# Column-tiled adaLN units placed behind the reads of the sample states

## The chip, the core and the metric

One NeuronCore of a Trainium2 chip runs the whole program. The metric is the device time of one execution in microseconds (us). TensorE is called PE, VectorE DVE, ScalarE ACT, GpSimd POOL; SP is the engine whose queue issues nearly all DMAs, in program order.

## The reference, cut to what matters

One decoder layer for 256 prompt tokens and 8 sample sequences of 8 tokens, all in float32:

```
mod = silu(c) @ w_ada + b_ada                        # adaLN: 9 rows of c, 6 x 2048 columns
h   = rmsnorm(x) * (1 + scale1) + shift1
proj = h @ w_in                                      # feeds both branches
GLA: S_t = diag(a_t) S_{t-1} + k_t^T v_t,  o_t = q_t S_t        # 4 heads, states 256 x 512
SSD: h_t = exp(dt_t A) h_{t-1} + dt_t x_t B_t^T,  y_t = h_t C_t # 8 groups, states 128 x 512
x = x + gate1 * ((sigmoid(gA) * yA + sigmoid(gB) * yB) @ w_mix_out)
x = x + gate2 * SwiGLU(rmsnorm(x) * (1 + scale2) + shift2)
```

The samples start from given states, so each of the 8 sequences has its own state per head or group, which is read (q S, or C h), updated and written back.

## The kernel before, in words

**Weights.** Every large product runs as "quads": a tile of 512 x 512 weights is loaded in two halves (`raw`, 512 KB each, `load_raw` line 162), split into a rounded part `whi` (ACT) and the rest `wlo` (DVE, `split_w` line 172), and multiplied in 48 matmuls of 320 columns: for each 128 x 128 block `whi` by the high and by the low part of the activations, then `wlo` by the high part (`quad_mm`, line 327). `raw` has 4 buffers, `whi` and `wlo` 3 each. `Stream.ahead` splits two halves ahead of the one in use.

**The order of the work.** PE's order is the order in which the program is written. Small work runs from generators: `Background.tick` (line 144) is called 8 times per quad, once after every 6 matmuls, and `yield n` lets n ticks pass before the next step. The order of the other engines and of SP is made by the compiler's scheduler, which also hands out the buffers as they come free. `bg.drain()` (line 894 for GLA, 1119 for SSD) runs what is left of a generator at once.

**adaLN units.** `mod` is made in units (class `Ada`, line 248). A unit loads 1 MB of `w_ada` into two of the four `raw` buffers (`load`) and multiplies it with `c` as the stationary operand, 32 columns wide, so that four matmuls of 512 columns run side by side in four column groups of the array (`mm`, line 274; tile `ad`). After four units ACT copies the sums to `adap`, and `flush` (line 294) transposes them with PE (tile `p`) and adds them up on DVE into `mod`. 36 units run at the start, 60 between quads from line 912 on: `ada_every[0] = 2` lets every second quad load one unit at its start and run it at its end. The last four run before the feed-forward part.

**Sample states.** Class `States` (line 599) has 10 buffers `st` of 256 KB. `read` multiplies four states with four stationary operands of 32 columns, in the same four column groups (tile `inter`); `update` runs one matmul (tile `upd`), adds it to the state on DVE and stores the state. `gla_work` (line 626) does four reads per head, each followed by four updates, a step every second tick; `ssd_work` (line 956) does two reads per group in the same way. The GLA part has 4 heads and runs beside the products of lines 882 to 908; the SSD part has 8 groups, whose work starts beside the z product of its group.

The profile shows one float32 matmul as two instructions, so that a read or a unit of four matmuls is "x8" there and "x4" in the program's order.

Of the kernel before, what the change touches and what calls it, by code (L numbers as in the profile page):

```python
# [60 lines left out]
def hybrid_kernel(tc, ctx, a, o):  # L61
# [14 lines left out]
    def stile(shape, dt=F32, name="s"):  # L76
        t = pool.tile(shape, dt, tag="s", bufs=N_S, name=name)
        return t
# [26 lines left out]
    def tt(eng, out, in0, in1, op):  # L105
        return eng.tensor_tensor(out=out, in0=in0, in1=in1, op=op)  # L106
# [141 lines left out]
    class Ada:  # L248
# [12 lines left out]
        def load(self, small=False, spare=False):  # L261
            if self.units:
# [8 lines left out]
                    raws = [load_raw(src[:, h * 1024:(h + 1) * 1024], spare or c < 8) for h in range(2)]  # L271
                self.loaded.append((c, b0, nb, q, raws))

        def mm(self):
            self.flush()
            if not self.loaded:
                return
            c, b0, nb, q, raws = self.loaded.pop(0)
            if q == 0:
                t = psum.tile([128, 512], F32, tag="ad", bufs=1, name="ad")  # L280
                self.ps = t
            w = 128 * nb
            m = 2048 // w
            n = m // len(raws)
            for j in range(m):
                T.matmul(self.ps[32 * (j % 4):32 * (j % 4) + 32, :w], c_s[:, m * q + j, :],
                         raws[j // n][:, (j % n) * w:(j % n) * w + w], start=q == 0 and j < 4,
                         stop=q == nb - 1 and j >= m - 4, tile_position=(0, 32 * (j % 4)))
            if q == nb - 1:
                part = stile([128, 512], name="adap")  # L290
                S.copy(part[:, :w], self.ps[:, :w])
                self.parts.append((c, b0, nb, part))
# [26 lines left out]
    ada = Ada()  # L319
# [29 lines left out]
    quad_no = [0]  # L349
    ada_every = [0]  # L350

    def gemm(names, quads, evac, apart=False):
        pss = [mm_ps() for _ in range(4)]
        n = len(names)
        for q in range(n):
            quad_no[0] += 1
            xq = quads(q) if callable(quads) else quads[q]
            quad_mm(pss, names[q], xq, q == 0, q == n - 1, evac,
                    1 if ada_every[0] and len(ada.units) > 4 and quad_no[0] % ada_every[0] == 0 else 0, apart,
                    (lambda: quads(q + 1)) if callable(quads) and q + 1 < n else None)  # L360


# [141 lines left out]
    def stack_k(ps, hf, n):  # L504

        R = pool.tile([96, n, 128], F32R, tag="k", bufs=3, name="R")
        src = ps[quarter(hf), 0:128 * n].rearrange("p (a b) -> p a b", a=n)
        S.copy(R[quarter(0)], src)
        S.copy(R[quarter(1)], src)
        tt(V, R[quarter(2)], src, R[quarter(hf)].bitcast(F32), ALU.subtract)  # L510
        return [stack_stationary(R[:, i]) for i in range(n)]
# [114 lines left out]
    def gla_work(H):  # L626
        hd, vT, KK, qe, kx = H.hd, H.vT, H.KK, H.qe, H.kx
        order = [(4 * hf + j, kb) for hf in range(2) for kb in range(2) for j in range(4)]
        states = States([a["S_gla"][hd, b, kb] for b, kb in order], [o["gla_s"][hd, b, kb] for b, kb in order])
        yield 6 if hd else 12  # L630
        states.load(4)
        yield 4

# [6 lines left out]
            T.transpose(ps[0:64, 128 * mb:128 * mb + 128], vT[:, mb, NP:], ident)  # L640
        S.copy(xs_tok[0:64], ps[0:64])
        hst = [stack_k(psK, hf, 2) for hf in range(2)]
        yield 4

        psA = ax_ps("inter")
        for n in range(4):
            hf, kb = divmod(n, 2)
            if kb == 0:
                mv = stack_v(xs_tok, hf)
            states.read(psA, [H.qpad[:, kb, 4 * hf + j] for j in range(4)], n, n == 0, n == 3)  # L650
            yield 1
            for j in range(4):
                tok = NP + 8 * (4 * hf + j) + 7

                def decay(st, ps, kb=kb, tok=tok):
                    V.scalar_tensor_tensor(out=st, in0=st, scalar=H.eb[:, kb, tok:tok + 1], in1=ps,
                                           op0=ALU.mult, op1=ALU.add)

                states.update(n, j, hst[hf][kb][:, j], mv, decay)
                yield 1  # L660
        inter = stile([128, 512], name="inter")
        S.copy(inter, psA)
        vt = []
# [245 lines left out]
    prev = heads[3]  # L909


    ada_every[0] = 2

    def conv_evac(ck, dst, cvs, cvo):
        def f(mb, pss):
# [31 lines left out]
    def bc8(x):  # L947
        return x.unsqueeze(2).to_broadcast([x.shape[0], 8, 64])

    def v8(x):  # L950
        return x.rearrange("p (h d) -> p h d", d=64)
# [4 lines left out]
    def ssd_work(W):  # L956
# [29 lines left out]
        xl = stile([64, 512], name="xl")  # L986
        tt(V, v8(xl), v8(ps[0:64]), bc8(dtL_tok[:, hsl]), ALU.mult)
        tt(V, v8(xs_tok[0:64]), v8(ps[0:64]), bc8(dt_tok[0:64, 2, hsl]), ALU.mult)
        yield 4

        psA = ax_ps("inter")
        for hf in range(2):
            mv = stack_v(xl, hf)
            states.read(psA, [cpad[:, 4 * hf + j] for j in range(4)], hf, hf == 0, hf == 1)
            for j in range(4):
                st = states.tiles[4 * hf + j]
                tt(G, v8(st), v8(st), bc8(ecs[:, :, 4 * hf + j]), ALU.mult)
            yield 1
            for j in range(4):
                states.update(hf, j, hst[hf][:, j], mv, lambda st, ps: tt(V, st, st, ps, ALU.add))  # L1000
                yield 1
        inter = stile([128, 512], name="inter")
        tt(V, v8(inter), v8(psA), bc8(ecs_r[:, hsl]), ALU.mult)

# [415 lines left out]
```

## Time and profile before

| | |
|---|---|
| median of 3 runs | 2940.89 us (2935.99 to 2942.86) |
| the profiled execution | 2946.89 us, its span 2945.1 us |
| PE busy | 2881.8 us, 98% of the span |
| PE weight loads busy | 2690.5 us |
| DVE, ACT, POOL busy | 1581.7, 1266.9, 360.3 us |
| mean granted TensorE clock | 0.994 |
| moved by DMA | 575.55 MB, mean 195 GB/s |

A matmul's record is longer than the step from one to the next, since matmuls overlap: a product of 320 columns is shown with 0.31 us and starts every 0.147 us. Costs on PE are therefore read as differences of start times. "Idle before" in a row begins only when the matmul before it has ended by its record.

### The profile page before, as it was taken

The numbers are of one execution on the slowest core, as the hardware profiler recorded it, in microseconds if no ns is written. First come the engines' busy times: TensorE is split into PE (matmuls) and PEld (weight loads), VectorE is DVE, ScalarE is ACT, GpSimd is POOL, SyncE is SP. The second block draws the span as 40 slices with busy tenths as digits, with TensorE's granted clock in tenths as the row PEclk, the third lists the DMA queues.
The fourth block names the chain that finished last, engine by engine and source line by source line (L and its number), as shares of the span: only waits on it lengthen the run. The fifth ranks groups of instructions, "written<-read, shape, count | busy, mean of one in ns | idle before, by whom it ended". The sixth has DMA issues, their size and how long they took to land.

```text
span 2945.1 us, 48524 instructions
## 1 busy us (share of the span) xinstructions
PE 2881.8 (98%) x19594; PEld 2690.5 (91%) x19594; DVE 1581.7 (54%) x2302; ACT 1266.9 (43%) x1991; POOL 360.3 (12%) x516
## 2 busy tenths in 40 slices
PE   7999999999999999999999999999999999999998
PEld 5898888998888889888888999999999999999998
DVE  5565565656656666666566544446344443444445
ACT  4344544345554554545455333435333233323333
POOL 0002111212322232322223000000000000000000
PEclk9999999999999999999999999999999999999999
DMA  9846636747667575775756644464444444444443
GB/s 386 323 137 236 203 134 209 233 161 275 239 213 241 202 252 192 240 238 201 243 195 238 210 167 161 168 217 138 150 151 150 149 149 150 149 150 150 151 150 115
DMA packets 181113, 575.55 MB, mean 195 GB/s; under 512 B 23252, under 2 KB 24600, under 8 KB 180888
## 3 DMA queue, kind: packets, MB, share of 16 engines
q1 hardware_dynamic: 180888, 572.45, 56.9%
q8 instruction: 154, 2.52, 0.3%
q14 instruction: 71, 0.58, 0.1%
HBM read 528.63 MB, written 43.74 MB: 194 GB/s over the span
## 4 chain that ended last, share of the span: by engine, by line
PE 86%; DMA 5%; DVE 5%; ACT 2%; issue 1%; SPq 0%; POOL 0%; ACTq 0%; DVEq 0%; POOLq 0%
PE mm L115 77%; DMA raw<-w_in 3%; PE ad L115 3%; DVE wlo L106 2%; ACT whi L132 1%; PE y L115 1%; PE fin L115 1%; PE upd L115 1%; DMA raw<-w_sp 1%; PE inter L115 1%; PE o L115 1%; DVE cacc L931 1%; DMA csb<-cs_d 1%; PE sum L115 0%; PE att L115 0%
## 5 line engine op out<-in xcount | busy, mean ns | idle before, releaser
L106 DVE TENSOR_TENSOR wlo<-raw,whi 128x1024 fp32r<-128x1024 f32 x712 | 883.1, 1242 | 949.6 <-ACT whi L132 934.6
L132 ACT CAST whi<-raw 128x1024 fp32r<-128x1024 f32 x712 | 746.0, 1048 | 1336.9 <-PE mm L115 1006.3
L115 PE MATMUL mm<-hh,whi 128*128 128x320 f32 x2560 | 812.4, 317 | 7.3 <-ACT whi L132 4.6
L115 PE MATMUL mm<-hh,wlo 128*128 128x320 f32 x2560 | 793.8, 310 | 9.3 <-DVE wlo L106 9.1
L115 PE MATMUL mm<-hl,whi 128*128 128x320 f32 x2560 | 791.8, 309 | 1.3 <-DVE hl L106 1.3
L115 PEld LDWEIGHTS mm<-hh,whi 128*128 128x128 f32 x2560 | 481.9, 188 | 86.1 <-issue 50.7
L115 PEld LDWEIGHTS mm<-hh,wlo 128*128 128x128 f32 x2560 | 481.9, 188 | 12.4 <-DVE wlo L106 12.1
L115 PEld LDWEIGHTS mm<-hl,whi 128*128 128x128 f32 x2560 | 482.5, 188 | 9.6 <-issue 2.9
L115 PE MATMUL mm<-gh,whi 128*128 128x320 f32 x1408 | 435.4, 309 | 0.8 <-ACT gh L1242 0.8
L115 PE MATMUL mm<-gl,whi 128*128 128x320 f32 x1408 | 435.6, 309 | 0.0
L115 PE MATMUL mm<-gh,wlo 128*128 128x320 f32 x1408 | 435.3, 309 | 0.0
L115 PEld LDWEIGHTS mm<-gh,whi 128*128 128x128 f32 x1408 | 264.3, 188 | 1.8 <-ACT gh L1242 1.8
L115 PEld LDWEIGHTS mm<-gl,whi 128*128 128x128 f32 x1408 | 264.3, 188 | 0.5 <-DVE gl L106 0.3
L115 PEld LDWEIGHTS mm<-gh,wlo 128*128 128x128 f32 x1408 | 264.3, 188 | 0.0
L115 PE MATMUL mm<-alo,whi 128*128 128x320 f32 x704 | 217.6, 309 | 0.0
L115 PE MATMUL mm<-ahi,whi 128*128 128x320 f32 x704 | 217.6, 309 | 0.0
L115 PE MATMUL mm<-ahi,wlo 128*128 128x320 f32 x704 | 217.6, 309 | 0.0
L106 POOL TENSOR_TENSOR ss<-ss,sq 128x320 f32<-128x320 f32 x14 | 12.1, 867 | 1410.6 <-ACT sq L109 1410.6
L115 PE MATMUL mm<-yhi,whi 128*128 128x320 f32 x512 | 171.6, 335 | 5.2 <-DVE yb L106 4.7
L115 PE MATMUL mm<-yhi,wlo 128*128 128x320 f32 x512 | 158.2, 309 | 0.0
L115 PE MATMUL mm<-ylo,whi 128*128 128x320 f32 x512 | 158.1, 309 | 0.0
L115 PEld LDWEIGHTS mm<-ahi,whi 128*128 128x128 f32 x704 | 132.2, 188 | 0.0
(279 smaller groups left out, 3635.1 us busy)
## 6 DMA issues: line engine op xcount, KB each, us to landing
raw<-w_in SPq DMA_DIRECT2D x320, 512.0 KB, 4.1
raw<-w_fi SPq DMA_DIRECT2D x176, 512.0 KB, 3.6
raw<-w_ada SPq DMA_DIRECT2D x120, 512.0 KB, 5.5
raw<-w_fo SPq DMA_DIRECT2D x88, 512.0 KB, 3.5
raw<-w_sp SPq DMA_DIRECT2D x64, 512.0 KB, 4.6
araw<-w_ada SPq DMA_DIRECT2D x52, 512.0 KB, 8.6
st<-S_gla SPq DMA_DIRECT2D x64, 256.0 KB, 5.0
gla_s<-st SPq DMA_DIRECT2D x64, 256.0 KB, 3.5
```

Source lines behind the costliest of these rows:

```text
L106: return eng.tensor_tensor(out=out, in0=in0, in1=in1, op=op)
L115: Tensor.last = nc.tensor.matmul(*args, **kw)
L132: first = S.copy(hi, src)
L931: V.scalar_tensor_tensor(out=av[:, 0:344], in0=u[:, k:k + 344], scalar=vec[:, cw + k:cw + k + 1], in1=av[:, 0:344], op0=ALU.mult, op1=ALU.add)
```

## The change

After each read of sample states one adaLN unit runs at once, in the GLA part too, where no unit ran before: 4 in each of the 4 heads and 2 in each of the 8 SSD groups, 32 in all. A new method `preload` loads a unit a few ticks ahead of the first read of a head or group, and the next unit directly behind the unit just run. `unit` is `mm` without the flush in front; the flush comes behind the first update that follows. The remaining 28 units run after every fourth quad in place of every second, and only when no preloaded unit waits. The updates of GLA take one tick more per read, those of SSD three ticks each in place of two; the GLA work of heads 1 to 3 begins four ticks earlier.

```diff
--- before.py
+++ after.py
@@ -271,8 +271,15 ...
                     raws = [load_raw(src[:, h * 1024:(h + 1) * 1024], spare or c < 8) for h in range(2)]
                 self.loaded.append((c, b0, nb, q, raws))
 
+        def preload(self):
+            if len(self.units) > 4 and not self.loaded:
+                self.load()
+
         def mm(self):
             self.flush()
+            self.unit()
+
+        def unit(self):
             if not self.loaded:
                 return
             c, b0, nb, q, raws = self.loaded.pop(0)
@@ -356,7 +363,7 ...
             quad_no[0] += 1
             xq = quads(q) if callable(quads) else quads[q]
             quad_mm(pss, names[q], xq, q == 0, q == n - 1, evac,
-                    1 if ada_every[0] and len(ada.units) > 4 and quad_no[0] % ada_every[0] == 0 else 0, apart,
+                    1 if ada_every[0] and len(ada.units) > 4 and quad_no[0] % ada_every[0] == 0 and not ada.loaded else 0, apart,
                     (lambda: quads(q + 1)) if callable(quads) and q + 1 < n else None)
 
 
@@ -627,7 +634,7 ...
         hd, vT, KK, qe, kx = H.hd, H.vT, H.KK, H.qe, H.kx
         order = [(4 * hf + j, kb) for hf in range(2) for kb in range(2) for j in range(4)]
         states = States([a["S_gla"][hd, b, kb] for b, kb in order], [o["gla_s"][hd, b, kb] for b, kb in order])
-        yield 6 if hd else 12
+        yield 2 if hd else 12
         states.load(4)
         yield 4
 
@@ -640,6 +647,7 ...
             T.transpose(ps[0:64, 128 * mb:128 * mb + 128], vT[:, mb, NP:], ident)
         S.copy(xs_tok[0:64], ps[0:64])
         hst = [stack_k(psK, hf, 2) for hf in range(2)]
+        ada.preload()
         yield 4
 
         psA = ax_ps("inter")
@@ -648,6 +656,9 ...
             if kb == 0:
                 mv = stack_v(xs_tok, hf)
             states.read(psA, [H.qpad[:, kb, 4 * hf + j] for j in range(4)], n, n == 0, n == 3)
+            ada.unit()
+            if n < 3:
+                ada.preload()
             yield 1
             for j in range(4):
                 tok = NP + 8 * (4 * hf + j) + 7
@@ -657,7 +668,9 ...
                                            op0=ALU.mult, op1=ALU.add)
 
                 states.update(n, j, hst[hf][kb][:, j], mv, decay)
-                yield 1
+                if j == 0:
+                    ada.flush()
+                yield 2 if j == 0 else 1
         inter = stile([128, 512], name="inter")
         S.copy(inter, psA)
         vt = []
@@ -909,7 +922,7 ...
     prev = heads[3]
 
 
-    ada_every[0] = 2
+    ada_every[0] = 4
 
     def conv_evac(ck, dst, cvs, cvo):
         def f(mb, pss):
@@ -986,19 +999,25 ...
         xl = stile([64, 512], name="xl")
         tt(V, v8(xl), v8(ps[0:64]), bc8(dtL_tok[:, hsl]), ALU.mult)
         tt(V, v8(xs_tok[0:64]), v8(ps[0:64]), bc8(dt_tok[0:64, 2, hsl]), ALU.mult)
+        ada.preload()
         yield 4
 
         psA = ax_ps("inter")
         for hf in range(2):
             mv = stack_v(xl, hf)
             states.read(psA, [cpad[:, 4 * hf + j] for j in range(4)], hf, hf == 0, hf == 1)
+            ada.unit()
+            if hf == 0:
+                ada.preload()
             for j in range(4):
                 st = states.tiles[4 * hf + j]
                 tt(G, v8(st), v8(st), bc8(ecs[:, :, 4 * hf + j]), ALU.mult)
             yield 1
             for j in range(4):
                 states.update(hf, j, hst[hf][:, j], mv, lambda st, ps: tt(V, st, st, ps, ALU.add))
-                yield 1
+                if j == 0:
+                    ada.flush()
+                yield 2
         inter = stile([128, 512], name="inter")
         tt(V, v8(inter), v8(psA), bc8(ecs_r[:, hsl]), ALU.mult)
 
```

**PE, at the first read of the GLA part** (`inter` is a read, `mm` the weight matmuls, `ad` the unit). One piece of the difference:

```order
 L115 MATMUL mm<-hh,wlo 128x320
 L115 MATMUL inter<-st,qpad 32x512 x4
+L115 MATMUL ad<-raw,c_s 32x512 x4
 L115 MATMUL mm<-hh,whi 128x320
 L115 MATMUL mm<-hl,whi 128x320
```

The unit now stands directly behind the read. Counted over the whole order, column-tiled stretches that other matmuls enclose (reads, units, or both joined) go from 121 to 93; four of the joined ones were there before.

**SP, around the first read of SSD group 1** (`raw<-w_ada` is half a unit, `raw<-w_in` half a weight tile, `st` the states, `csb` a table of 640 KB that this group needs). Before:

```order
L167 DMA raw<-w_ada 128x1024
L936 DMA conv_o<-cvo 128x108
L610 DMA st<-S_ssm 128x512 x4
L967 DMA csb<-cs_d 128x1280 x2
L167 DMA raw<-w_ada 128x1024
L167 DMA raw<-w_in 128x1024 x2
L610 DMA st<-S_ssm 128x512 x4
L167 DMA raw<-w_in 128x1024 x2
```

And now:

```order
L949 DMA conv_o<-cvo 128x108
L617 DMA st<-S_ssm 128x512 x4
L980 DMA csb<-cs_d 128x1280 x2
L167 DMA raw<-w_in 128x1024
L167 DMA raw<-w_ada 128x1024 x2
L167 DMA raw<-w_in 128x1024
L167 DMA raw<-w_ada 128x1024
L617 DMA st<-S_ssm 128x512 x4
L167 DMA raw<-w_ada 128x1024
L167 DMA raw<-w_in 128x1024
```

Both halves of the unit now stand behind the tables and behind one weight half; the next unit and four states stand ahead of a later weight half. In the even groups the weight half that here stands right behind `csb` stands ahead of the states, where half a unit stood before.

**SP, between the second and the third read of GLA head 1** (`gla_s` are stores of states). Before:

```order
L624 DMA gla_s<-st 128x512
L610 DMA st<-S_gla 128x512 x4
L624 DMA gla_s<-st 128x512
L526 DMA d_3383<-d 128x320
L167 DMA raw<-w_in 128x1024
L624 DMA gla_s<-st 128x512
```

And now:

```order
L631 DMA gla_s<-st 128x512
L617 DMA st<-S_gla 128x512 x4
L167 DMA raw<-w_ada 128x1024 x2
L631 DMA gla_s<-st 128x512
L167 DMA raw<-w_in 128x1024
L631 DMA gla_s<-st 128x512 x2
```

A unit's 1 MB now stands between the states and the next weight half.

## Rows read from the trace of the kernel before

**Rows 1.** The page: span, and busy time of each engine (share of the span, instructions).

```profile
span 2945.1 us, 48524 instructions
...
PE 2881.8 (98%) x19594; PEld 2690.5 (91%) x19594; DVE 1581.7 (54%) x2302; ACT 1266.9 (43%) x1991; POOL 360.3 (12%) x516
```

**Rows 2.** Who waited for whom, PE, from 680 to 1600 us (the SSD part): total us, times, longest.

```profile
PE mm L115 <- DVE wlo L106: 9.1, 10, 1.5
...
PE mm L115 <- ACT whi L132: 4.6, 6, 1.4
```

**Rows 3.** The same, from 200 to 680 us (the GLA part): the longest of all, and the longest of a weight product.

```profile
PE sum L115 <- POOL ss L106: 2.0, 1, 2.0
...
PE mm L115 <- ACT ohi L132: 1.1, 1, 1.1
```

**Rows 4.** PE in order of time, at the first GLA read: start us, us, instruction.

```profile
239.59 0.31 PE L115 MATMUL mm<-hh,wlo 128*128 128x320 f32 x1
239.83 1.06 PE L115 MATMUL inter<-st,qpad 128*32 128x512 f32 x8
240.82 0.41 PE L115 MATMUL mm<-hh,whi 128*128 128x320 f32 x1
241.07 0.30 PE L115 MATMUL mm<-hl,whi 128*128 128x320 f32 x1
```

**Rows 5.** The same, at the first unit behind a quad.

```profile
630.40 0.31 PE L115 MATMUL mm<-hh,wlo 128*128 128x320 f32 x1
630.64 1.07 PE L115 MATMUL ad<-raw,c_s 128*32 128x512 f32 x8
631.63 0.41 PE L115 MATMUL mm<-hh,whi 128*128 128x320 f32 x1
631.88 0.30 PE L115 MATMUL mm<-hl,whi 128*128 128x320 f32 x1
```

**Rows 6.** The same, at the first read of SSD group 1, which a unit followed directly (in brackets: idle before, and what ended it).

```profile
801.59 0.31 PE L115 MATMUL mm<-hh,wlo 128*128 128x320 f32 x1
801.83 1.06 PE L115 MATMUL inter<-st,cpad 128*32 128x512 f32 x8
802.71 1.04 PE L115 MATMUL ad<-raw,c_s 128*32 128x512 f32 x8
804.85 0.41 PE L115 MATMUL mm<-hh,whi 128*128 128x320 f32 x1 [1.10 <-ACT whi L132]
...
806.22 0.42 PE L115 MATMUL mm<-hh,wlo 128*128 128x320 f32 x1 [0.81 <-DVE wlo L106]
```

**Rows 7.** The loads of the stationary operand of units: ns min/median/max, first and last start us, forms.

```profile
L115 PEld LDWEIGHTS ad<-raw,c_s x480: 106/109/111, 630.6 to 1678.6; 128*32 128x32 f32 x160
```

**Rows 8.** ACT in order of time, at the same read of SSD group 1.

```profile
803.75 1.04 ACT L132 CAST whi<-raw 128x1024 fp32r<-128x1024 f32 x1 [0.69 <-PE ad L115]
805.06 1.04 ACT L132 CAST whi<-raw 128x1024 fp32r<-128x1024 f32 x1 [0.27 <-DMA raw<-w_in]
```

**Rows 9.** SP in order of time, ahead of it (the time is that of the issue alone).

```profile
792.69 0.90 SPq L967 DMA_DIRECT2D csb<-cs_d  x2
793.69 0.38 SPq L167 DMA_DIRECT2D raw<-w_ada  x1
794.46 1.43 SPq L167 DMA_DIRECT2D raw<-w_in  x2
795.94 3.00 SPq L610 DMA_DIRECT2D st<-S_ssm  x4
```

**Rows 10.** DMA issues from 794.4 to 795.7 us: KB each, median us from issue to landing.

```profile
raw<-w_in SPq DMA_DIRECT2D x2, 512.0 KB, 9.3
```

**Rows 11.** The page: the two instructions that split a weight half (busy us, mean ns of one, idle before).

```profile
L106 DVE TENSOR_TENSOR wlo<-raw,whi 128x1024 fp32r<-128x1024 f32 x712 | 883.1, 1242 | 949.6 <-ACT whi L132 934.6
L132 ACT CAST whi<-raw 128x1024 fp32r<-128x1024 f32 x712 | 746.0, 1048 | 1336.9 <-PE mm L115 1006.3
```

**Rows 12.** DMA issues from 228 to 284 us (the reads of GLA head 0): KB each, median us to landing.

```profile
raw<-w_in SPq DMA_DIRECT2D x9, 512.0 KB, 6.3
```

**Rows 13.** The same from 430 to 490 us (head 2).

```profile
raw<-w_in SPq DMA_DIRECT2D x13, 512.0 KB, 4.7
```

**Rows 14.** Busy time by stretch: the stretch, its us, busy us of PE, its weight loads, DVE, ACT, POOL, granted clock, share of the DMA engines' time, GB/s. The first is between two reads of head 0, the second between two of head 1, the last two are other stretches of heavy loading.

```profile
250.77:261.72 10.95, 10.95 (x73) 9.71 (x73) 5.61 (x7) 2.14 (x3) 0.00 (x0) 1.00 0.93 322
...
348.70:359.70 11.00, 11.00 (x74) 9.72 (x74) 8.64 (x12) 4.38 (x9) 0.00 (x0) 1.00 0.80 263
...
20.00:60.00 40.00, 36.68 (x295) 28.26 (x288) 20.15 (x39) 21.22 (x41) 0.52 (x1) 0.96 1.02 400
...
803.70:806.30 2.60, 0.69 (x7) 0.38 (x3) 1.47 (x2) 2.09 (x2) 2.60 (x3) 1.00 1.07 406
```

**Rows 15.** PE in order of time, an update and the weight matmul behind it.

```profile
242.68 0.40 PE L115 MATMUL upd<-mv,hs 96*128 96x512 f32 x1
242.92 0.31 PE L115 MATMUL mm<-hh,whi 128*128 128x320 f32 x1
```

**Rows 16.** The updates of the GLA states on DVE: ns min/median/max, first and last start us.

```profile
L656 DVE SCALAR_TENSOR_TENSOR st<-st,ge,upd x64: 740/747/749, 243.7 to 595.5; 128x512 f32<-128x512 f32 x64
```

## What the change should do, written before it ran

> **What bounds the kernel now.** Read first the page: PE is busy for 98% of the span, DVE for 54% [rows 1]. Only what PE does, or waits for, can move the time. Second, read who waited for whom. In the SSD part PE waits for split weights, 9.1 us for `wlo` and 4.6 us for `whi` in 16 waits, none over 1.5 us [rows 2]; in the GLA part no weight product waits for more than 1.1 us [rows 3]. Third, read PE in order of time where it leaves the weight matmuls. A lone read costs more than its own work: the last weight matmul ahead of it starts at 239.59, the second behind it at 241.07, which is 1.48 us for two ordinary steps of 0.147 and the read, so 1.19 us [rows 4]. A lone unit costs the same, 630.40 to 631.88 [rows 5]. Where a unit follows a read directly, it starts 0.88 us after the read [rows 6], and not after the 0.99 us plus a slow step that weight matmuls need. The change in and out of the column-tiled form is paid once for both.
>
> **The profiled execution.** It took 2946.9 us, 6.0 above the median of 2940.9. Terms are summed against the former; the forecast is the median plus the sum.
>
> **Term 1, joining: -8.7 us.** Joined, read and unit take 0.24 (into the read) + 0.88 + 0.99 (unit to the next weight matmul) + 0.25 (to the second), less two steps of 0.147: 2.07 us [rows 4 to 6]. Apart they take 2 x 1.19 = 2.38. One join saves 0.31 us. The order holds 32 joined pairs; 4 stood there before, and in 4 more only a flush lay between, so column-tiled stretches go from 121 to 93. 28 x 0.31 = 8.7 us, all on PE, which nothing covers. The number of units, and with it what they load, stays.
>
> The four column groups share their rows, and a load of a unit's stationary operand takes 109 ns [rows 7]; the unit at 802.71 began 0.88 us after its read, as two passes of the read take, so its first four loads ran beside the read [rows 6]. The Trainium skill, "TensorE: Matmul & The Clock Gate", Part 3, The mechanism, says against this that weight loads run beside matmuls in flight only where their row groups differ. The trace does not bear that out here; what it would cost is rival (d).
>
> **Term 2, units in the GLA part: +3 us.** Sixteen units come to where none ran. Their PE time only moves here from later. What is new is that from the first preload of a head to its last unit, some 45 us, two of the four `raw` buffers belong to units, and weight halves go through the other two. In the order a weight half that takes a buffer which a unit gives back is used 48 to 60 matmuls and three updates later: 48 x 0.147 + 3 x 0.24 = 7.8 us at least [rows 15]. It needs a landing, 4.7 us by the median in head 2 and 6.3 in head 0 [rows 12, 13], a `whi` of 1.05 and a `wlo` of 1.24 [rows 11]: 7.0 to 8.6 us. The spare time is -0.8 to +0.8 us, where the kernel before had four buffers and no such wait [rows 3]. One half per head is worse placed: its load stands behind the store of a state, which waits for an update's 0.75 us on DVE [rows 16], and 7.0 us are left. I take one late half of 0.75 us per head, 3 us. The ends are 0 (all land as in head 2) and 16 x 0.8 = 13 us (all as in head 0).
>
> The DMA engines are what sets those landings. Between two reads of head 0 they are 93% busy, so 10.2 of 10.95 us, in head 1 80% [rows 14]. A unit adds 1 MB, 2.6 us at the 400 GB/s of heavy loading [rows 14]. The interval grows by the unit's 0.88 us on PE and one tick, 6 x 0.147 = 0.88, to 12.7; that tick uses a quarter of a weight half, 0.3 us more of loading. So the engines are needed for 13.1 of 12.7 us at the fullest, and for 8.8 + 2.9 = 11.7 at a common interval: at the bound in the one, a microsecond short of it in the other. Neighbours share a queue, so I add nothing for it here; it is rival (b).
>
> **Term 3, the first read of an SSD group: +3.8 us.** Before, in group 1, the weight matmul behind read and unit starts at 804.85 where 802.71 + 0.99 = 803.70 was possible, and the third of them at 806.22, another 1.07 late [rows 6]. Together 2.2 us, where the rows show 1.10 + 0.81 idle. The reason is the queue: unit half, two weight halves and four states are issued behind two `csb` tables [rows 9], the two weight halves land 9.3 us after their issue [rows 10], and their splits start as they land, at 803.75 and 805.06, one landing every 1.31 us [rows 8]. Scaled by 2.2 / 1.9, the 13.7 us of rows 2 are some 15.8 us on PE.
>
> Now one weight half stands first behind `csb` and lands at about 802.4, the two unit halves at 803.7 and 805.0. Weights are no longer late, but the unit is: it could start at 802.71, its second half must wait until 805.0, so it is 2.3 us late. The next unit and four states then stand ahead of a later weight half: 805.0 + 1.3 (a weight half) + 1.3 (half a unit) + 2.6 (states) + 1.3 (the other half) + 1.3 = 812.8; split by 812.8 + 1.05 + 1.24 = 815.1. It is wanted 9.8 us after the read plus the 2.3, at 813.9, and its `wlo` 0.3 later: 0.9 us late. In even groups the first weight half stands ahead of the states, so each unit half lands a step sooner: 1.25 us late, then some 0.4. After: 4 x 3.2 + 4 x 1.65 = 19.4 us, against 15.8: +3.6, and 0.2 for flushes that now come closer behind their unit. The ends: if every landing comes a step of 1.3 us sooner, only the odd groups' units are late, 4 x 1.0, which is -11.8; a step later in every group is 8 x 1.3 more, +14.
>
> **Term 4, the rest: +0.4 us.** The loop of head 0 is four ticks longer without an earlier start, so its last update falls into the drained stretch behind it. It moves 0.24 us of PE and 0.75 of DVE there [rows 15, 16]; 0 to 0.75. The wider updates cost PE nothing: each is the same matmul, and DVE has room. The SSD work ends a quad later, still ahead of its drain. Fewer units beside the other quads save nothing, since nothing waited there.
>
> **Sum.** -8.7 + 3 + 3.8 + 0.4 = -1.5 us: 2939.4. About 0.2% (5.9 us) is what a measurement of this kernel tells from no change.
>
> **Rivals.** (a) *The weights keep up.* Landings stay near 4.7 us in GLA and the SSD queue costs what it cost before. Then only terms 1 and 4 count, -8.3: 2932.6; with part of the SSD waits gone, 2930. For it: DVE has room, and beside the units of ordinary SSD quads two free buffers were enough, since rows 2 show only 16 waits in 920 us. Against it: the 9.3 us landings [rows 10]. Chance 0.33. (b) *The transfers bound the GLA reads* (the side of slower). Where the DMA engines need longer for an interval than PE, every weight half comes later by the excess. It decides where they move this mixture at the rate of the fullest interval, 322 / 0.93 = 346 GB/s, and not at 400: 1.18 MB then cost 3.4 us, the interval 13.6, 0.9 more than PE needs, and landings go to those of head 0 or beyond. Term 2 is then its end of 13, term 3 stays: +8.5, 2949.4. For it: 93% busy already [rows 14]. Against it: heads 1 to 3 have more room, and less than half of the intervals are that full. Chance 0.18. (c) *What I forecast*, the joins paid back by late units and late weights: 0.47. (d) *A unit's loads wait for the read.* Then a join exposes 4 x 0.109 = 0.44 us and saves 0.31, so term 1 is 28 x 0.13 = +3.6, the sum +10.8, 2951.7. Only rows 6 speak on it, and against it: 0.02.
>
> That the joins do not happen is no rival: the order shows them.
>
> **How the numbers follow.** The likeliest is (c), 2939.4, by its own terms 2934 to 2946. The range takes in (a) to 2930 and most of (b): 2930 to 2950. Faster by over 0.2% is (a), 0.33; within 0.2%, (c), 0.47; slower, (b) and (d), 0.20. All terms at their lower or all at their upper ends together I leave out.
>
> **What would show it.** Right: a unit starting 0.4 us or more after its place behind an SSD read while its `raw` lands; no more lone reads; first weight matmuls behind SSD reads that don't wait; some waits for `whi` and `wlo` between 230 and 600 us, of 3 us in all. Wrong: SSD units that start 0.88 us after the read and run through (term 3 too high, rival a); GLA intervals of over 13 us with DMA shares near 1.0 (rival b); a joined pair that takes 2.3 us with its data there (term 1).

## The result and the profile after

The changed kernel takes 2979.1 us (median of 4 runs, 2978.9 to 2990.0), the kernel before 2941.9 beside it: 1.0135 times as long, 95% interval 1.0119 to 1.0150. The forecast was 2939.4, its range ended at 2950. The profiled run took 2978.9 us.

The page after, which answers to [rows 1]: the span is 31.8 us longer, PE is busy for a smaller share of it, and DVE does the same work.

```profile
span 2976.9 us, 48432 instructions
...
PE 2891.6 (97%) x19594; PEld 2707.5 (91%) x19594; DVE 1580.9 (53%) x2302; ACT 1268.4 (43%) x1991; POOL 379.5 (13%) x516
```

What PE waited for after, from 200 to 680 us (total us, times, longest). In [rows 3] no weight product waited for `whi` or `wlo` for more than 1.1 us; now they lead the list.

```profile
PE mm L115 <- ACT whi L132: 8.6, 5, 3.2
PE mm L115 <- DVE wlo L106: 6.1, 8, 1.3
```

The same from 680 to 1620 us, against [rows 2]: the waits for `wlo` went from 9.1 us with none over 1.5 to 22.3 with the longest 2.4.

```profile
PE mm L115 <- DVE wlo L106: 22.3, 14, 2.4
PE mm L115 <- ACT whi L132: 4.6, 4, 2.5
```

PE after, in order of time, at the first read of SSD group 1, the place of [rows 6]. From the last weight matmul ahead of the pair to the second behind it are 2.35 us, less two steps of 0.147: 2.06. The unit starts 0.88 us after the read and does not wait; the wait comes 10 us behind the pair.

```profile
836.50 0.31 PE L115 MATMUL mm<-hh,wlo 128*128 128x320 f32 x1
836.74 1.06 PE L115 MATMUL inter<-st,cpad 128*32 128x512 f32 x8
837.62 1.04 PE L115 MATMUL ad<-raw,c_s 128*32 128x512 f32 x8
838.60 0.42 PE L115 MATMUL mm<-hh,whi 128*128 128x320 f32 x1
838.85 0.31 PE L115 MATMUL mm<-hl,whi 128*128 128x320 f32 x1
...
848.59 0.41 PE L115 MATMUL mm<-hh,wlo 128*128 128x320 f32 x1 [1.55 <-DVE wlo L106]
```

**An account of lost time.** Totals of waits by their rows do not add up to the span, since a matmul's record overlaps the next. So all of PE's start times were added up: between two weight matmuls everything over the step of 0.147 us is lost, and where other work stands between, what it costs is the way from the last weight matmul ahead to the second behind, less two steps. A step longer by 0.06 to 0.2 us is counted as slow clock, a longer one as a wait, a smaller difference not at all. All these kernels have the same 17,088 weight matmuls in the same order, so a stage is a stretch of that count (GLA 1,151 to 3,120, SSD to 8,500, then the end). The sums, in us:

| kernel | GLA: waits, slow clock, other work | SSD: waits, slow clock, other work | start + end | all |
|---|---|---|---|---|
| before | 0.3, 3.8, 113.2 | 19.1, 4.1, 190.8 | 65.8 | 397.0 |
| after | 16.2, 7.3, 129.2 | 25.6, 12.9, 163.9 | 74.3 | 429.6 |

The difference, 32.6, is that of the spans (31.8) within a microsecond. "Other work" moved in the main as it was ordered: 16.0 us more in GLA and some 6 at the end, where more units run now, and 26.9 less in SSD. Some lateness hides in it: 3 us at joined pairs of GLA, and 7.5 us at updates of SSD, of which the 58 that stand alone cost 21.6 us where 0.24 each would be 13.9. What made the kernel slower is waits (+22.8) and slow clock (+12.2 over all stages).

**Where the new SSD wait stands.** Seven times, once in each of the groups 1 to 7, PE waits 2.1 to 2.5 us for one `wlo`, always at the first product behind the convolution product that follows a projection. These are 16.8 of the 25.6 us. DVE after, in order of time, at the fourth of them (a row of several instructions gives the start of the first and the time to the end of the last):

```profile
1172.75 1.48 DVE L1119 SCALAR_TENSOR_TENSOR xs<-xs,vec,rstd 128x320 f32<-128x320 f32 x3
1174.14 1.30 DVE L106 TENSOR_TENSOR ylo<-xs,yhi 128x320 fp32r<-128x320 f32 x3
1175.37 0.54 DVE L1119 SCALAR_TENSOR_TENSOR xs<-xs,vec,rstd 128x320 f32<-128x320 f32 x1
1175.83 1.21 DVE L106 TENSOR_TENSOR wlo<-raw,whi 128x1024 fp32r<-128x1024 f32 x1
1176.96 0.49 DVE L106 TENSOR_TENSOR ylo<-xs,yhi 128x320 fp32r<-128x320 f32 x1
1177.38 0.82 DVE L941 TENSOR_SCALAR cacc<-u,vec 128x344 f32<-128x344 f32 x2
1178.12 3.00 DVE L944 SCALAR_TENSOR_TENSOR cacc<-u,vec,cacc 128x344 f32<-128x344 f32 x6
1181.05 0.82 DVE L941 TENSOR_SCALAR cacc<-u,vec 128x344 f32<-128x344 f32 x2
1181.78 3.00 DVE L944 SCALAR_TENSOR_TENSOR cacc<-u,vec,cacc 128x344 f32<-128x344 f32 x6
1184.71 3.48 DVE L106 TENSOR_TENSOR wlo<-raw,whi 128x1024 fp32r<-128x1024 f32 x3
```

ACT and PE at the same place:

```profile
1180.18 1.05 ACT L132 CAST whi<-raw 128x1024 fp32r<-128x1024 f32 x1 [3.20 <-DMA raw<-w_in]
...
1183.47 0.31 PE L115 MATMUL mm<-hl,whi 128*128 128x320 f32 x1
1185.97 0.41 PE L115 MATMUL mm<-hh,wlo 128*128 128x320 f32 x1 [2.20 <-DVE wlo L106]
```

The `whi` is there at 1181.2, early enough for a `wlo` of 1.2 us before PE wants it at 1183.6. But DVE works in its order: the normalisation of the group (`xs`, `ylo`, `ssd_finish`) runs until 1177.4, the sixteen steps of the convolution's evacuation (`cacc`) only then, and `wlo` behind them at 1184.7. In the kernel before, the last `ylo` of this group starts 14.1 us ahead of the product's first weight matmul; here 6.4. This one distance sorts all the kernels of this text, those of the experiments below included: in six of them (the changed one, e2, e3, e4, e7 and e8) it is 4.6 to 6.9 us in every one of the seven groups, and each has all seven waits, of 2.1 to 4.5 us; in the other nine it is 12.5 to 15.2 us, and none waits there for more than 1 us.

**What a wait can cost besides.** Busy time by stretch, with the granted clock as the third number from the end: about a microsecond after that wait PE runs for 3.5 us at 0.51 of full speed, the lower of its two levels (1.2 GHz), though it is busy throughout; its steps are 0.267 us there. The third row is the stretch behind the sixth of the seven waits, 2.4 us long too, where the clock stayed up.

```profile
1186.90:1190.40 3.50, 3.50 (x16) 3.50 (x15) 1.29 (x2) 0.00 (x0) 1.36 (x1) 0.51 0.80 242
1190.40:1200.00 9.60, 9.60 (x67) 9.60 (x67) 3.44 (x3) 3.15 (x3) 0.00 (x0) 1.00 0.55 186
...
1434.20:1440.20 6.00, 5.95 (x40) 5.96 (x41) 3.49 (x3) 1.07 (x2) 2.33 (x1) 1.00 0.69 223
```

From 680 to 1620 us the granted clock falls eight times, for 3.4 us or once for 6.8, at a loss of 1.2 to 1.7 us each; in the kernel before once. Four of the eight stand at or behind the end of one of the seven long waits, the other four near shorter ones, and three of the seven long waits have none. So the length of one wait does not decide it alone; what does is not shown.

**Where the GLA waits stand.** SP after, in order of time, around the third read of head 2. The store at 485.11 is followed by four states (1 MB), a unit (1 MB), and only at 489.85 by the weight half that PE needs.

```profile
485.11 0.33 SPq L631 DMA_DIRECT2D gla_s<-st  x1
485.50 2.36 SPq L617 DMA_DIRECT2D st<-S_gla  x4
488.79 0.81 SPq L167 DMA_DIRECT2D raw<-w_ada  x2
489.85 0.33 SPq L167 DMA_DIRECT2D raw<-w_in  x1
```

ACT and PE there: the half has landed when its `whi` starts at 497.43, 7.6 us after its issue (4.7 was the median in head 2 before, [rows 13]).

```profile
497.43 1.04 ACT L132 CAST whi<-raw 128x1024 fp32r<-128x1024 f32 x1 [6.50 <-DMA raw<-w_in]
...
498.53 0.42 PE L115 MATMUL mm<-hh,whi 128*128 128x320 f32 x1 [1.98 <-ACT whi L132]
```

Two stretches around it (last two numbers: share of the DMA engines' time, GB/s): over 20 us the engines are busy for 96% and move 342 GB/s, and in the 13 us that matter without a gap, at 365.

```profile
478.00:498.00 20.00, 18.13 (x121) 15.67 (x119) 8.80 (x13) 2.66 (x3) 0.48 (x1) 1.00 0.96 342
...
485.00:498.00 13.00, 11.13 (x75) 8.82 (x73) 4.70 (x6) 2.66 (x3) 0.00 (x0) 1.00 1.00 365
```

### The profile page after: what moved, and what is told of

The parts are those of the page before. It is cut to its first block, busy times and chain, and to the rows that moved or that the text cites. A ratio compares the mean times of both kernels' runs of the same rounds, so it can differ in the third digit from the quotient of the medians.

```text
span 2976.9 us, 48432 instructions
## 1 busy us (share of the span) xinstructions
PE 2891.6 (97%) x19594; PEld 2707.5 (91%) x19594; DVE 1580.9 (53%) x2302; ACT 1268.4 (43%) x1991; POOL 379.5 (13%) x516
## 4 chain that ended last, share of the span: by engine, by line
PE 89%; DVE 5%; DMA 4%; ACT 1%; issue 1%; SPq 0%; POOL 0%; DVEq 0%; ACTq 0%; POOLq 0%
PE mm L115 79%; DMA raw<-w_in 4%; PE ad L115 2%; DVE wlo L106 2%; PE y L115 1%; DVE cacc L944 1%; PE inter L115 1%; PE fin L115 1%; PE upd L115 1%; PE o L115 1%; ACT whi L132 1%; PE sum L115 0%; PE att L115 0%; DMA araw<-w_ada 0%; DMA araw<-w_adf 0%
## 5 line engine op out<-in xcount | busy, mean ns | idle before, releaser
L115 PE MATMUL mm<-hh,whi 128*128 128x320 f32 x2560 | 823.2, 322 | 16.2 <-ACT whi L132 13.2
L115 PE MATMUL mm<-hh,wlo 128*128 128x320 f32 x2560 | 802.9, 314 | 28.5 <-DVE wlo L106 28.4
L115 PEld LDWEIGHTS mm<-hh,whi 128*128 128x128 f32 x2560 | 488.6, 191 | 93.6 <-issue 38.7
L115 PEld LDWEIGHTS mm<-hh,wlo 128*128 128x128 f32 x2560 | 488.7, 191 | 34.9 <-DVE wlo L106 34.9
L115 PEld LDWEIGHTS mm<-hl,whi 128*128 128x128 f32 x2560 | 488.8, 191 | 8.4 <-issue 2.9
L115 PEld LDWEIGHTS mm<-alo,whi 128*128 128x128 f32 x704 | 132.2, 188 | 0.0
```

What stands on the lines that cost most here:

```text
L115: Tensor.last = nc.tensor.matmul(*args, **kw)
```

## The experiments

Theory A for SSD: the wider updates end a group's work later, so that its normalisation meets the convolution's evacuation on DVE. Its rival B: a preloaded unit holds the `raw` buffers that the late half needs. For GLA: the units' loads, by their bytes or by the buffers they hold, against the units' PE time and the earlier start. The ratios are to the kernel before on the same chip, with 95% intervals; lost time as in the table above.

| kernel | ratio | GLA: waits, slow, other | SSD: waits, slow, other | all |
|---|---|---|---|---|
| e1_ssd_close | 1.0042 (1.0027 to 1.0057) | 17.6, 8.3, 128.7 | 10.1, 1.3, 169.2 | 408.6 |
| e2_spread_only | 1.0126 (1.0095 to 1.0156) | 0.2, 3.8, 113.1 | 35.8, 13.6, 202.0 | 434.1 |
| e3_no_gla_units | 1.0227 (1.0195 to 1.0259) | 0.8, 3.6, 111.7 | 24.5, 14.6, 240.1 | 460.3 |
| e4_raw5 | 1.0060 (1.0045 to 1.0075) | 10.0, 5.9, 133.3 | 19.5, 4.5, 165.8 | 415.1 |
| e5_wide_early | 1.0083 (1.0060 to 1.0106) | 17.5, 6.8, 128.8 | 10.3, 3.3, 179.2 | 418.6 |
| e6_ssd_joins | 1.0018 (1.0005 to 1.0030) | 0.0, 4.1, 112.0 | 9.2, 4.4, 192.3 | 401.8 |
| e7_no_load | 1.0061 (1.0042 to 1.0081) | 0.0, 3.8, 126.3 | 28.3, 11.4, 168.2 | 410.9 |
| e8_other_bufs | 1.0236 (1.0209 to 1.0263) | 0.5, 5.1, 162.8 | 29.1, 15.5, 176.7 | 475.0 |
| e9_joins_raw5 | 0.9971 (0.9955 to 0.9986) | 0.0, 1.5, 115.0 | 4.8, 1.0, 181.3 | 386.5 |
| e10_before_raw5 | 0.9982 (0.9970 to 0.9993) | 0.5, 1.4, 114.8 | 2.4, 0.2, 196.0 | 381.9 |
| e11_half_gla | 1.0017 (1.0008 to 1.0026) | 0.5, 1.3, 118.9 | 9.6, 4.5, 190.4 | 394.7 |
| e12_pool_stores | 1.0099 (1.0086 to 1.0113) | 23.9, 10.3, 135.5 | 9.5, 1.2, 171.6 | 424.8 |
| e13_half_raw5 | 0.9966 (0.9950 to 0.9981) | 0.0, 2.6, 123.6 | 3.2, 1.7, 183.0 | 384.8 |

**e1_ssd_close.** The updates of SSD one tick apart again.

```diff
                 if j == 0:
                     ada.flush()
-                yield 2
+                yield 1
```

> The changed kernel with the updates of SSD one tick apart again; the joins, the preloads and the GLA part stay. Theory A (the wider updates put the normalisation of a group, some 5 us of DVE, into the evacuation of the next convolution product, so that one wlo per group comes 2.4 us late): the seven waits of 2.1 to 2.5 us at the second product behind a projection go, 16.8 us, and with them the half-clock stretches behind them, some 8 us; the time falls by about 24 us to 2953 to 2958. Theory B (a preloaded unit holds the raw buffer that this half needs): the seven waits stay, the time stays within 5 us of 2979. Both: the waits of the GLA part, 18.8 us, stay as they are.

2956.5 us. All seven waits are gone, SSD loses 21.9 us less (15.5 of waits and 11.6 of slow clock, against 5.3 more of other work). Theory A holds, B falls. DVE in e1, at the place shown above, where the product's first weight matmul starts at 1176.42: the sixteen steps begin 10.1 us ahead of it in place of 5.9, and three `wlo` stand between them (two of them shown).

```profile
1166.35 0.46 DVE L941 TENSOR_SCALAR cacc<-u,vec 128x344 f32<-128x344 f32 x1 [1.73 <-ACT u L935]
...
1173.61 1.22 DVE L106 TENSOR_TENSOR wlo<-raw,whi 128x1024 fp32r<-128x1024 f32 x1
...
1175.23 1.22 DVE L106 TENSOR_TENSOR wlo<-raw,whi 128x1024 fp32r<-128x1024 f32 x1
```

One cost appeared in place of the waits. In e1 the unit behind the first read of group 1 waits for its second half to land, as the prediction had it:

```profile
837.01 1.06 PE L115 MATMUL inter<-st,cpad 128*32 128x512 f32 x8
838.04 1.05 PE L115 MATMUL ad<-raw,c_s 128*32 128x512 f32 x4
839.32 1.05 PE L115 MATMUL ad<-raw,c_s 128*32 128x512 f32 x4 [0.23 <-DMA raw<-w_ada]
```

Over the sixteen SSD pairs that is 9.2 us more than 16 x 2.05, in the changed kernel 0.6: there the wait of 2.4 us ahead of the pairs gave the loads the time that they lacked. Other runs agree: e5, without that wait, has 8.1 us, e4, which keeps it, 0.4.

**e2_spread_only.** The kernel before with the wider SSD updates, nothing else.

```diff
                 states.update(hf, j, hst[hf][:, j], mv, lambda st, ps: tt(V, st, st, ps, ALU.add))
-                yield 1
+                yield 2
```

> The kernel before with one edit: the updates of SSD two ticks apart; no join, no unit in the GLA part. Theory A: the same waits of 2.1 to 2.5 us for wlo show up once in each of seven groups, with their half-clock stretches: +20 to +25 us over the kernel before, less up to 8 us if the waits for yb go, so 2955 to 2965. Theory B: no unit is preloaded here, so no such waits, and 2942 within 5 us.

2982.7 us, more than expected. No unit is preloaded and nothing joined, and the waits are there, at the same seven weight matmuls, 2.4 to 4.3 us each. This one number in the diff is enough to make the kernel 1.3% slower. The waits for `yb` did not go (4.3 us in four).

**e3_no_gla_units.** No unit in GLA, and its old start; in `gla_work`:

```diff
-        yield 2 if hd else 12
+        yield 6 if hd else 12
...
-        ada.preload()
...
-            ada.unit()
-            if n < 3:
-                ada.preload()
...
-                if j == 0:
-                    ada.flush()
-                yield 2 if j == 0 else 1
+                yield 1
...
-    ada_every[0] = 4
+    ada_every[0] = 2
```

> The changed kernel without units in the GLA part; its reads stand alone and start where they did before, and the 44 other units go after every second quad. The GLA waits for split weights (18.8 us against 1.4 before) and the half clock behind them (2 us) should go, less 16 joins of 0.31 us: -14 us in all, 2965 within 5. If the earlier start or something else of the change made the GLA weights late, the waits stay and the time is 2979 + 5. The seven waits at the second product behind a projection stay by theory A (wider updates), and are fewer by theory B if other units stand elsewhere.

A miss of the edit, 3008.7 us: with units after every second quad, a read took the unit that its quad had loaded, and the quad's end then ran the one just preloaded, which had yet to land. In SSD the first read with its units cost 6 to 12 us in each group. Only its GLA part can be read, and there this edit takes back the earlier start and the longer updates along with the units: 0.8 us of waits are left, so the waits come from these edits; which of them makes them only e7 tells.

**e4_raw5.** Five `raw` buffers; the space comes from `w` and `n`.

```diff
-            raw = stage.tile([128, 1024], F32, tag="raw", bufs=4, name="raw")
+            raw = stage.tile([128, 1024], F32, tag="raw", bufs=5, name="raw")
...
-            w = pool.tile([128, 384], F32, tag="w", bufs=4, name="w")
+            w = pool.tile([128, 384], F32, tag="w", bufs=2, name="w")
...
-N_N = 5
+N_N = 4
```

> The changed kernel with five raw buffers in place of four; the space is taken from the small work (two buffers w of SSD in place of four, four n in place of five), so only the GLA part is to be read. If the GLA weights are late because two of four raw buffers belong to units, a third free buffer takes most of the 18.8 us of waits away: 6 us or less between 230 and 640 us. If the DMA engines or ACT and DVE are what is late, the waits stay at 15 to 19 us. For the SSD part: theory B says the seven waits of 2.4 us shrink too, theory A says they stay; fewer w buffers may add waits of their own there.

The seven SSD waits stay, 2.4 to 2.8 us each, as theory A said; the other SSD waits, those behind the first reads, shrink from about 8 us to 2. In GLA 10.0 us stay, between what the two theories wanted: the buffer is a part of it. By head the waits are 2.1, 0.0, 4.9 and 3.1 us, where the changed kernel has 5.8, 4.5, 3.6 and 2.4. So the fifth buffer helps heads 0 and 1; in heads 2 and 3, where the late halves are 7.5 to 7.8 us on their way, it does not bring them in time.

**e5_wide_early.** The wide updates kept, the four output steps of a group closer.

```diff
                                    in1=ps[:, :NT], op0=ALU.mult, op1=ALU.add)
-            yield 4
+            yield 2
```

> The changed kernel with the wide updates of SSD kept, and the four output steps of each group two ticks apart in place of four, so that a group's work ends about as early as in the kernel before. If what costs is that the work ends later and its normalisation meets the convolution's evacuation on DVE, the seven waits of 2.1 to 2.5 us go and the time falls by some 20 us, to about 2959. If it is the spacing of the updates itself (the states are held and stored later), they stay: 2979 within 5.

The seven waits go (10.3 us of waits in SSD, as with close updates), so it is the end of the work that decides and not the spacing. The time fell by less than expected. The closer output steps are dearer: with the eight units that now stand right behind one they cost 58.5 us, in the changed kernel, apart, 48.9; in seven groups such a step together with its unit costs 3.3 us.

**e7_no_load.** The 16 GLA units multiply a resident tile and load nothing; their part of adaLN is left out.

```diff
-                    raws = [load_raw(src[:, h * 1024:(h + 1) * 1024], spare or c < 8) for h in range(2)]
+                    raws = [cst[:, 0:512]] * 4 if resident else [load_raw(src[:, h * 1024:(h + 1) * 1024], spare or c < 8) for h in range(2)]
...
-        ada.preload()
+        ada.preload(True)
...
```

> The changed kernel, but the 16 units of the GLA part multiply a resident tile and load nothing, so their part of adaLN is left out; their matmuls and the joins stay. If the loads are what makes the weights late in GLA, the waits there (16.2 us) fall below 2 us, the half clock to the 3.8 us of before, and the interludes to 16 x 2.05 + the rest: -20 us, 2959. If the units' PE time or the earlier start is the cause, the waits stay above 10 us.

No GLA wait is left, and the slow clock is that of before. The loads are the cause, with the buffers that they hold; 22.7 us of lost time hang on them, of 16 MB. The units' PE time and the earlier start, which e7 keeps, are not.

**e8_other_bufs.** The GLA units load into four tiles of 256 KB of another pool.

```diff
-        def preload(self):
+        def preload(self, small=False):
             if len(self.units) > 4 and not self.loaded:
-                self.load()
+                self.load(small=small)
...
-        ada.preload()
+        ada.preload(True)
...
```

> The changed kernel, but the 16 units of the GLA part load into four small tiles of 256 KB of another pool, so that they move the same bytes and hold no raw buffer. If buffers are the cause of the GLA waits, they fall to 3 us or less (five raw buffers left 10.0). If the traffic or the order of the queue is the cause, 8 to 16 us stay. The tiles come from a pool of ten that the small work shares; if that pool runs short, new waits show at the reads instead.

The weight halves are on time (0.5 us), and the units wait instead, 22.8 us in 15 waits for their own loads. It tells less than it should, since the pool of ten that holds these tiles may have run short.

**e11_half_gla.** Units at the second and fourth read of a GLA head only, close updates.

```diff
-            ada.unit()
-            if n < 3:
+            if n % 2:
+                ada.unit()
+            else:
                 ada.preload()
...
-    ada_every[0] = 4
+    ada_every[0] = 3
```

> The changed kernel with close SSD updates and units at the second and fourth read of each GLA head only, loaded right behind the read before: 8 units in GLA in place of 16, the other units after every third quad. If the traffic of states and units bounds the intervals between reads (342 GB/s at 96% of the DMA engines between 478 and 498 us of the changed kernel), half the units bring the GLA waits from 16.2 to 4 us or less, and the half clock to about 5. If holding two raw buffers is enough by itself, each remaining unit keeps its share: 8 us. The time: 2935 to 2945 by the first, 2945 to 2952 by the second.

0.5 us of waits, not half of 17.6. The loss is not one per unit but sets in between 8 and 16 units. Half the units are half the bytes and also hold buffers for about half the time, so this does not tell the two apart. The time is above the first theory's, because of SSD, which loses 204.5 us in place of e1's 180.6: more of the other units run there, and units and updates behind the first reads are late again.

**e12_pool_stores.** e1 with the stores of GLA states issued by POOL.

```diff
-            nc.sync.dma_start(self.dsts[i], self.tiles[i])
+            (nc.gpsimd if len(self.srcs) == 16 else nc.sync).dma_start(self.dsts[i], self.tiles[i])
```

> The changed kernel with close SSD updates (2956.5 us, GLA waits 17.6) and the stores of GLA states issued by POOL in place of SP. If a weight half is late because its issue stands in SP's queue behind a store that waits for an update (as at 485 us), the GLA waits fall to 8 us or less. If it is the traffic, the bytes are the same and the waits stay at 14 to 20 us.

The waits rise to 23.9 us, so with no store ahead of it in SP's queue a half is no earlier. SP in e12 shows what it waits for instead: it issues nothing for eleven microseconds, with a unit's half next in line.

```profile
481.96 1.29 SPq L167 DMA_DIRECT2D raw<-w_in  x2
494.25 0.33 SPq L167 DMA_DIRECT2D raw<-w_ada  x1
494.67 1.81 SPq L617 DMA_DIRECT2D st<-S_gla  x4
496.58 0.75 SPq L167 DMA_DIRECT2D raw<-w_ada  x1
497.38 14.44 SPq L167 DMA_DIRECT2D raw<-w_in  x4
```

With no store to hold it back, SP runs ahead until the unit's half finds no free `raw` buffer, and states and weights stand behind it. DVE there gives a buffer back just ahead of that issue: a `wlo`, the last to read its `raw`, ends at 494.21.

```profile
492.99 1.22 DVE L106 TENSOR_TENSOR wlo<-raw,whi 128x1024 fp32r<-128x1024 f32 x1 [5.95 <-ACT whi L132]
```

That the buffer is what SP waited for is inferred from this and from what stands first in line. The Trainium skill, "DMA: Bandwidth & Descriptors", section Issuing engines are not separate DMA queues, says that transfers of all issuing engines run on the same 16 DMA engines, so that a second issuer saves issue time only. The run agrees in so far as the second issuer gained nothing: a weight half still took 6.3 us to land from 485 to 510 us, and the kernel is slower than e1.

**The versions that follow from this.** e6: joins in SSD alone, close updates, other units every third quad, a quad's own unit left out where the read took it. e9: the same with five `raw` buffers. e10: the kernel before with five. e13: e11 with five.

```diff
+        mine = None
         if n_ada:
             ada.load()
+            mine = ada.loaded[-1]
...
-        if n_ada:
+        if mine is not None and mine in ada.loaded:
             ada.mm()
```

> Joins in SSD alone: updates one tick apart, no unit and no earlier start in GLA, and the other units after every third quad (a quad's own unit is left out where the read has taken it; this avoids the second unit that waited 6 to 10 us for its data at the first read of each group when units went after every second quad). By what the runs show so far, lost time in GLA goes to 116 us as before (152.8 changed), in SSD to some 190 (180.6 with close updates, 8 more lone units of 1.19), at the end to some 22: about 382 us against 397.0 before, so 0.5% faster than before, 2927 to 2937 where the kernel before takes 2942 to 2946. If joins as such bring nothing in SSD (the weight halves behind the reads are late again), no difference from before.

> Joins in SSD alone (close updates, nothing in GLA, other units after every third quad) with five raw buffers (space from w, four to two, and n, five to four). In the run with four buffers 9.2 us of waits and some 10 us of late units and updates stood around the first read of each group. If a preloaded unit's hold on two of four buffers is their cause, five take most of both: lost time in SSD from 206 to about 190, the whole 2930 to 2938, 0.3% faster than before. If it is the order of the queue (states and units ahead of the weight half) or the traffic, the waits stay and the time is that of four buffers, 0.2% slower than before.

> The kernel before with the same five raw buffers: what the buffer alone brings. Its SSD waits are 19.1 us, most of them right behind reads with a unit; if the buffers cause them, 10 us or more go: 2932 to 2936. If the 9.3 us landings behind tables and states cause them, less than 4 us go and the two or four lost small buffers may cost as much: 2940 to 2946.

> Close SSD updates, units at the second and fourth read of each GLA head, the other units after every third quad, and five raw buffers. With four buffers this lost 120.7 us in GLA, 204.5 in SSD and 15.9 at the end. If the rest of the loss at the first SSD reads is the hold on the buffers, as five buffers showed for the joins in SSD alone (206 to 187 us), SSD comes to 186 to 190 and the whole to 2928 to 2934, the fastest of these kernels. If eight more units beside GLA states need the fourth buffer for another reason than traffic, or if joins save nothing where nothing is late, it is no faster than the kernel before with five buffers, 2937.

e6 is 0.2% slower than before, not faster: the waits in SSD fell by 9.9 us, but late units and updates took their place (other work 192.3 us). With the fifth buffer these go too. In e9 and e13 every joined pair costs 2.05 us, and the waits of weight matmuls in SSD are 4.8 and 3.2 us, most of which is not for split weights (3.6 us for `z` in e9). Their medians are 2936.5 and 2937.2 us beside 2943.2 and 2944.9. But e10, without any new join, has 2937.2 on the chip of e9 beside the same 2943.2, 0.6 more than e9; its ratio is 0.9982, its SSD waits fall from 19.1 to 2.4 us, and the three intervals overlap. The gain is the buffer's as far as is shown. What the joins add, 3 to 5 us by the middles of the ratios and nothing by the lost time of the profiles, was not shown, and e13's time is the one that its expectation gave for joins that save nothing. The space it takes costs something as well: with two `w` in place of four the 32 output steps of SSD cost 49.9 us in e10 against 39.4 before.

## Why the prediction was wrong

**Term 1, joining, -8.7 us: right.** A joined pair costs 2.05 us and a lone read or unit 1.19, so 0.33 per join. Rival (d), the loads that wait for the read, does not occur.

**Term 2, units in GLA, +3 us: the mechanism right, the size wrong.** I took one late half of 0.75 us per head; measured are 2.4 to 5.8 us of waits per head, in all +15.9 us of waits and +3.5 of slow clock. Rival (b) had the case, and nearly the condition: it decides where the busy engines move the mixture at 346 GB/s rather than 400; from 478 to 498 us they moved 342 at 0.96 of their time, so 356 while busy, and 365 in the 13 us without a gap. Its price was term 2's end of 13. The step that failed is the size, and with it "neighbours share a queue, so I add nothing for it here": 8 units cost 0.5 us of waits where 16 cost 16. That two intervals in a row have no slack left for each other fits this, but was argued and not shown. The shares of held buffers and of bytes stay open: a fifth buffer takes 6 of 16 us, half the units, which is half of both, takes all.

**Term 3, the first SSD read, +3.8 us: right as a mechanism, hidden by another.** It said late units, then late weights, 19.4 us in all. The changed kernel shows units that wait for nothing (0.6 us) and some 8 us of late weights. e1, without the wait in front, shows 9.2 us of late units and 10.1 of waits: 19.3. That the sum is met is in part luck, since the term had 14.2 of late units and 5.2 of late weights. The 15.8 taken for the kernel before are some 14 by the same account, so the loss over it is some 5 us in place of 3.6.

**Term 4, the rest, +0.4 us: this step failed.** "The wider updates cost PE nothing: each is the same matmul, and DVE has room. The SSD work ends a quad later, still ahead of its drain." The reasons given hold, and the conclusion does not. I asked whether the drain would catch the work, and not which other work of DVE its new end would meet. By e1 the wider updates cost 21 us of lost time net of what they hid, by e2 37 us when made alone. A mean of 54% [rows 1] hides that DVE is full for the 12 us from the normalisation to the end of the evacuation, and it works in order. What the runs show in place of "cost PE nothing": the last `ylo` moved from over 12 us to under 7 ahead of the next product's first weight matmul, the evacuation began behind it and the `wlo` behind the evacuation, and PE waited 2.1 to 2.5 us seven times.

**The clock, in no term.** Slow clock, most of it in stretches at 1.2 GHz behind waits, cost 12 us more over the kernel than before. In SSD there was one such stretch before, eight in the changed kernel and one in e1, so they went with the waits, though not one by one.

The sum of what was forecast rightly (terms 1 and 3, -4.9) with what was measured for GLA (+19.4) is +14.5; e1, which has just these, lost 11.6 us more than before.

## What to carry to other kernels

When work is moved later, look up what each in-order engine does at its new end, not only at its new place: a mean busy share says nothing on a burst, and the one short instruction behind it may be what PE needs. Price transfers over a run of intervals, since a stage that is just at the bound in each may have no slack to lend; and vary the dose, as half may cost nothing. An account of lost time by stage, from start times, shows which part of a change with several edits is to be undone.

## What the runs showed of the hardware

After a single wait of PE, 2.2 us of idle time by its row, the granted clock fell to 0.51, and not at once: PE worked at full speed for about a microsecond, then at half for 3.5 us, then in full again. Behind three of the seven such waits it stayed at 1.00, and it also fell behind shorter waits. The DMA engines moved a mixture of loads and stores at 365 GB/s with no gap from 485 to 498 us, less than the 400 and 406 of [rows 14]. A joined read and unit cost 2.05 us in every one of the 24 pairs of e13, where two apart cost 2.38.
